# Retention loop: spreading the second split of the hidden planes over two tiles, and preparing the conv weights one tile earlier

## The chip, the cores and the metric

One core of one Trainium2 chip runs the kernel. The metric is device time in microseconds, the median of several executions. The engines are PE (TensorE, the matmuls), DVE (VectorE), ACT (ScalarE), POOL (GpSimd) and SP (SyncE, which here only issues DMAs). ACT issues some DMAs too. Each engine works through its own instructions in one fixed order; waits are semaphores.

## The reference, cut to what matters

One decoder layer on 2048 tokens of width 1024, in float32:

```python
mod = silu(c) @ ada_w + ada_b            # shift, scale, gate, two of each
h = x * (1 + scale_m) + shift_m
z = h @ w_in                              # 3*512 conv columns, 4*512 retention columns
y_conv = bg * conv3(cg * xin)             # short causal convolution
q, k = rotary(q), rotary(k) * d**-0.5     # 4 heads of 128, chunks of 128 tokens
y_ret = silu(g) * groupnorm(retention(q, k, v))
x = layernorm(alpha * x + gate_m * (concat(y_conv, y_ret) @ w_out))
h = x * (1 + scale_f) + shift_f
x = layernorm(alpha * x + gate_f * ((silu(h @ w_gate) * (h @ w_up)) @ w_down))
```

## The kernel before, in words

Float32 matmuls are made of fp16 ones. A helper `split` (L129 to L131) turns a float32 tile into a high and a low fp16 half: ACT writes the high half (L130), DVE the low one (L131). `mm3` (L135 to L137) makes one product of three fp16 matmuls, so most of PE's time has these three lines.

The retention half runs over 16 tiles of 128 tokens (`for t in range(4, NT)`; the first four tiles stand in the startup). `gemm_ret(t, u)` makes one of four column groups of 512 (v, q, k, gate) with 24 matmuls; its eviction from PSUM is DVE L709 for u = 0, ACT L713 for u = 1 and 2 and ACT L715 for u = 3. `evicted[0]` is the last of these, and `tc.issue_after(evicted[0])` asks that what follows is issued behind it. `rotary` is DVE L738 to L740 and POOL L741, L742. The split of q and k (L130/L131 `128x512`) feeds two DMA transposes on SP (L757), which the scores and the keys' products on PE need one tile later (`ret_scores`, `ret_kv`). `ret_y` and `ret_part` norm the output of a tile (DVE L804 to L814, POOL L808 to L811, L127).

Every second tile ACT modulates the next 256 tokens (`ret_h`, L296) and `ret_hsplit` splits them into a page of planes `h` (L130/L131 `hs`, `128x1024`). The convolution half multiplies the same tokens by a scheme with seven products in place of eight, which needs sums of the planes. `h_more` makes them: `h_sums` on POOL (L344 to L347, in place), a second `h_split` into a page `g`, and then seven stores to `hcscr` that ACT issues (`h_store`, L356). `h_again` does this for the first token pairs, whose x is loaded again. Both are `chores`, one taken at the end of a tile; the stores lie in a list and are taken behind `gemm_ret(t, 1)` of the next tile. The planes come back as `hp_load` (SP, L952).

The conv half runs in units n (`conv_pair`: products 0, 5, 4, 1, 3, 6, 2 of 12 matmuls each, evictions ACT L975 and L979 and DVE L977 to L988; L979 is `e5`). Its weights are loaded (`cw_load`, L862), their maximum taken (`cw_max`, DVE L87, PE L99, DVE L104), scaled (ACT L884), subtracted on POOL (L885 to L888) and split (ACT L892, DVE L893) in `cw_split`, for unit u + 1 while unit u runs. DVE L1166 adds two pages of `w_out`, which come by SP L1157.

In the startup `ret_half_max(0, 1)` is a maximum over 2048 columns (DVE L87 to `m`), and `start_bound` computes a bound `mh` (DVE L286, L87, L291) that PE L99 needs. Before the channel half, the last two rows of the output projection are normed (DVE L1276, L1277, POOL L1279 to L1286, ACT L1289) while `gu(0, 1)` starts; `gu_split2` prepares its weights (DVE L1435 to L1437, ACT L1440, DVE L1441), ACT L1478, L1483 and L1487 are its evictions, and DVE L1492 an addition from PSUM.

## Time and profile before

| | |
|---|---|
| time, median of 3 runs | 2091.64 us (2090.89 to 2095.92) |
| profiled execution | 2092.12 us, its span 2090.3 us |
| granted TensorE clock, mean | 0.99 |
| busy: PE, DVE, POOL, ACT | 96%, 70%, 43%, 32% |

The span is the time between the first and the last instruction that the profiler records; 1.8 us lie around it. A busy share is an average over stages that differ: it does not say which engine is waited for in one of them. A granted clock of 1.00 is 2.4 GHz, of 0.50 is 1.2 GHz.

### The profile page before, as it was taken

To read this page: it belongs to the slowest core of one execution; us is meant where nothing else is said; L and a number is where in the kernel's file an instruction comes from. 1 tells how busy PE (TensorE), PEld (TensorE's weight loads), DVE (VectorE), ACT (ScalarE), POOL (GpSimd) and SP (SyncE) were. 2 spreads that over 40 slices of the span, in tenths; PEclk is the share of its full clock that TensorE was granted. 3 is DMA by queue.
4 is the path that set the end of the run, shared out by engine and by line. 5 is a ranking of instruction groups with operands and counts; after the bars stand their busy time and mean duration, and the time that the engine had idled before them with its cause. 6 is when DMAs were issued, how large, how long until landed. Compare 5 with 4: busy or idle time off the path is not lost.

```text
span 2090.3 us, 24590 instructions
## 1 busy us (share of the span) xinstructions
PE 2017.0 (96%) x9631; PEld 945.5 (45%) x9631; DVE 1467.6 (70%) x1796; ACT 666.6 (32%) x728; POOL 897.0 (43%) x748
## 2 busy tenths in 40 slices
PE   8899998889899999899999999999999999999998
PEld 4355554444344444344444444444444444444443
DVE  7897766768677577867677677877877353477564
ACT  5523425334322223433232223433433121212210
POOL 3555546655642377644223115444444043134332
PEclk9999999999999999999999999999999999999999
DMA  9046553596774198742354543443343765465321
GB/s 382 26 137 187 157 171 121 147 317 208 269 287 151 66 258 189 192 132 91 142 187 155 191 181 121 166 136 131 130 154 125 251 254 193 149 259 196 147 81 71
DMA packets 189491, 361.05 MB, mean 173 GB/s; under 512 B 118080, under 2 KB 118080, under 8 KB 166592
## 3 DMA queue, kind: packets, MB, share of 16 engines
q1 hardware_dynamic: 181168, 344.55, 49.4%
q10 hardware_dynamic: 8208, 14.95, 2.0%
q8 instruction: 75, 1.23, 0.2%
q14 instruction: 40, 0.33, 0.0%
HBM read 231.26 MB, written 100.93 MB: 159 GB/s over the span
## 4 chain that ended last, share of the span: by engine, by line
PE 41%; DVE 9%; DMA 5%; POOL 4%; issue 2%; ACT 2%; SPq 0%; POOLq 0%; DVEq 0%; ACTq 0%
PE mm L135 7%; PE mm L137 7%; PE mm L136 7%; PE ax L135 7%; PE ax L137 7%; PE ax L136 7%; DMA pg<-yscr 2%; DMA pg<-in_w_dn_dram 2%; DVE pg L1639 1%; DVE pg L1504 1%; DVE wdm L87 1%; DVE pg L1441 1%; DVE pg L1640 1%; ACT pg L1289 1%; DVE pg L1499 1%
## 5 line engine op out<-in xcount | busy, mean ns | idle before, releaser
L135 PE MATMUL mm<-pg,pg 128*128 128x512 f16 x1604 | 609.0, 381 | 23.9 <-ACT pg L713 5.4
L136 PE MATMUL mm<-pg,pg 128*128 128x512 f16 x1604 | 611.1, 381 | 0.0
L137 PE MATMUL mm<-pg,pg 128*128 128x512 f16 x1604 | 609.8, 380 | 0.0
L135 PE MATMUL ax<-pg,pg 128*128 128x512 f16 x1220 | 463.2, 380 | 8.3 <-ACT pg L892 4.5
L136 PE MATMUL ax<-pg,pg 128*128 128x512 f16 x1220 | 463.2, 380 | 0.0
L137 PE MATMUL ax<-pg,pg 128*128 128x512 f16 x1220 | 462.1, 379 | 0.6 <-DVE pg L893 0.6
L136 PEld LDWEIGHTS <-pg 128*128 128x128 f16 x2888 | 283.5, 98 | 357.5 <-issue 31.4
L135 PEld LDWEIGHTS <-pg 128*128 128x128 f16 x2888 | 283.5, 98 | 343.8 <-ACT pg L892 11.6
L137 PEld LDWEIGHTS <-pg 128*128 128x128 f16 x2888 | 283.4, 98 | 341.4 <-issue 10.8
L1497 POOL TENSOR_TENSOR pg<-pg,t2k 128x512 f32<-128x512 f32 x44 | 59.9, 1362 | 385.4 <-DVE t2k L1496 219.8
L131 DVE SCALAR_TENSOR_TENSOR pg<-pg,p2s,pg 128x2048 f16<-128x2048 f32 (+1 forms) x42 | 93.1, 2225 | 137.5 <-ACT pg L130 137.4
L130 ACT ACTIVATE pg<-pg,p2s 128x2048 f16<-128x2048 f32 (+1 forms) x42 | 77.5, 1858 | 262.3 <-PE mm L136 105.1
L87 DVE TENSOR_REDUCE m<-pg 128x2 bf16<-128x2048 f32 (+1 forms) x38 | 86.4, 2276 | 16.1 <-DMA pg<-in_w_gu_dram 12.5
L528 PE MATMUL mm<-pg,pg 128*128 128x512 f16 x384 | 88.5, 384 | 5.7 <-DVE pg L536 2.5
L1503 ACT ACTIVATE pg<-t2k,ivg 128x512 f32<-128x512 f32 x44 | 31.6, 718 | 180.9 <-DVE t2k L1502 169.6
L1552 DVE TENSOR_TENSOR pg<-pg,pg 128x2048 f16<-128x2048 f32 (+1 forms) x22 | 46.3, 2104 | 44.5 <-ACT pg L1551 44.5
L1425 DVE TENSOR_TENSOR pg<-pg,pg 128x2048 f16<-128x2048 f32 x22 | 52.2, 2371 | 29.2 <-ACT pg L1424 29.2
L1551 ACT ACTIVATE pg<-pg 128x2048 f16<-128x2048 f32 (+1 forms) x22 | 37.3, 1697 | 99.7 <-DMA wscr<-pg 63.0
L1279 POOL TENSOR_SCALAR rs<-mv 128x1 f32<-128x1 f32 x32 | 30.2, 948 | 82.5 <-DVE mv L1277 79.8
L131 DVE SCALAR_TENSOR_TENSOR pg<-pg,hs,pg 128x1024 f16<-128x1024 f32 x32 | 50.2, 1593 | 18.4 <-ACT pg L130 18.3
L1605 POOL TENSOR_TENSOR pg<-pg,pg 128x2048 f32<-128x2048 f32 (+1 forms) x6 | 27.0, 4492 | 82.0 <-DVE pg L131 38.6
L528 PEld LDWEIGHTS <-pg 128*128 128x128 f16 x384 | 37.4, 99 | 52.0 <-issue 6.9
(283 smaller groups left out, 2766.8 us busy)
## 6 DMA issues: line engine op xcount, KB each, us to landing
pg<-wscr SPq DMA_DIRECT2D x28, 1024.0 KB, 4.9
pg<-in_w_gu_dram SPq DMA_DIRECT2D x22, 1024.0 KB, 4.9
uscr<-pg SPq DMA_DIRECT2D x44, 512.0 KB, 3.0
pg<-in_w_dn_dram SPq DMA_DIRECT2D x22, 1024.0 KB, 6.3
pg<-in_adaT_dram SPq DMA_DIRECT2D x21, 1024.0 KB, 8.1
wscr<-pg SPq DMA_DIRECT2D x77, 256.0 KB, 2.9
yscr<-pg SPq DMA_DIRECT2D x16, 1024.0 KB, 4.2
pg<-uscr SPq DMA_DIRECT2D x16, 1024.0 KB, 5.4
```

The source lines that it names most:

```text
L87: return nc.vector.tensor_reduce(dst, src, axis=AX.X, op=OP.max, apply_absolute_value=True).ins
L130: nc.scalar.activation(hi, src, AF.Copy, scale=s)
L131: nc.vector.scalar_tensor_tensor(lo, src, s, hi, op0=OP.mult, op1=OP.subtract)
L135: nc.tensor.matmul(ps, l_hi, r_hi, start=start, stop=False, skip_group_check=again)
L136: nc.tensor.matmul(ps, l_hi, r_lo, start=False, stop=False, skip_group_check=again)
L137: return nc.tensor.matmul(ps, l_lo, r_hi, start=False, stop=stop, skip_group_check=again).ins
L528: nc.tensor.matmul(ps, hv[:, a, k, o], w[:, k], start=n == 0 and k == k0, stop=n == 2 and k == k1 - 1)
L1425: nc.vector.tensor_sub(wa[:, 2048:], pg, wa[:, :2048])
L1497: nc.gpsimd.tensor_add(e5, e5, p1)
L1503: nc.scalar.activation(u[:, 1], u2, AF.Silu, scale=iv_g)
L1551: nc.scalar.activation(o[:, :n, 0], src, AF.Copy)
L1552: nc.vector.tensor_sub(o[:, :n, 1], src, o[:, :n, 0])
```

## The change

- `h_more` is cut into three steps. The sums stay at the tile's end. The second split moves into a list `sums`, taken behind the next tile's `gemm_ret(t, 1)` (after its latest eviction). The stores follow at the end of that tile, before the next chore.
- `cw_load(0)` and `cw_max(0)` move one tile earlier (tile 14), `cw_load(1)` with them. `cw_split` is cut behind the POOL subtractions; the rest, `cw_finish`, is called from within `conv_pair` behind the eviction `e5` of the unit before.
- In the startup `ret_half_max(0, 1)` moves behind the two `start_bound`.
- `gu_split2(1)` moves from the last rows of the output projection to behind `gu(0, 1)`, to be issued after the eviction `e5` (L1483).

```diff
@@ -381,18 +381,21 @@
         else:
             chores.append(lambda: h_more(p, pg, h))
 
-    chores, stores = [], []
+    chores, sums, stores = [], [], []
 
     def h_more(p, pg, h, *done):
         h_sums(pg)
-        g, _ = h_split(pg, hs[:, 0:1])
-        free(pg)
-
-        def store():
-            h_store(p, h, (0, 1, None, 3))
-            h_store(p, g, (5, 2, 6, 4))
-            free(g, *done)
-        stores.append(store)
+
+        def parts():
+            g, _ = h_split(pg, hs[:, 0:1])
+            free(pg)
+
+            def store():
+                h_store(p, h, (0, 1, None, 3))
+                h_store(p, g, (5, 2, 6, 4))
+                free(g, *done)
+            stores.append(store)
+        sums.append(parts)
 
     def h_again(p):
 
@@ -651,9 +654,9 @@
             ret_xmax(p, KG, KT)
         start_all(2, 0, (0,))
         start_mod(1)
-        ret_half_max(0, 1)
         start_bound(1, 0)
         start_bound(1, 1)
+        ret_half_max(0, 1)
         start_all(2, 0, (1,))
         start_scale(1, 0, lambda: start_x(1, 0))
         start_scale(1, 1, lambda: start_x(1, 1))
@@ -872,6 +875,8 @@
                 cw[u][m] = v[:, i]
         cw[u]["tmp"] = owner[id(pg)][1][:, 1536:2048]
 
+    cw_parts = {}
+
     def cw_split(u):
         pg = cw_stage.pop(u)
         s = col(1, "s")
@@ -886,6 +891,10 @@
         nc.gpsimd.tensor_sub(f[:, 1], f[:, 3], f[:, 1])
         nc.gpsimd.tensor_sub(sv[:, 1], f[:, 3], sv[:, 0])
         nc.gpsimd.tensor_sub(sv[:, 2], f[:, 2], sv[:, 1])
+        cw_parts[u] = (pg, f, sv)
+
+    def cw_finish(u):
+        pg, f, sv = cw_parts.pop(u)
         cw_views(u)
         for i, (src, n) in enumerate(((f, 4), (sv[:, :3], 3))):
             o = cw[u]["pages"][i].rearrange("p (s a n) -> p s a n", s=4, a=2)[:, :n]
@@ -951,7 +960,7 @@
         hp[b, m] = page(F16)
         nc.sync.dma_start(hp[b, m], hcscr[b][m].rearrange("p j m -> p (j m)"))
 
-    def conv_pair(u, b, done=lambda m: None):
+    def conv_pair(u, b, done=lambda m: None, between=None):
         w = cw[u]
         iv = ivc[:, u:u + 1]
         kind, c = CONV[u]
@@ -976,7 +985,10 @@
         prod(pb, 5, True, True)
         nc.vector.scalar_tensor_tensor(u2, pb, iv, p1, op0=OP.mult, op1=OP.add)
         prod(pc, 4, True, True)
-        nc.scalar.activation(e5, pc, AF.Copy, scale=iv)
+        read = nc.scalar.activation(e5, pc, AF.Copy, scale=iv).ins
+        if between:
+            with tc.issue_after(read):
+                between()
         prod(pa, 1, False, True)
         pd = new()
         prod(pd, 3, True, True)
@@ -1082,12 +1094,12 @@
         if t == 4:
             xt_load(p, 1)
         end = t == NT - 1
+        if t == NT - 2:
+            cw_load(0)
         ret_transpose(t - 1)
         gemm_ret(t, 0)
         if end:
             free(*ret_pages[0:2])
-            cw_load(1)
-            cw_max(0)
         if t > 4:
             ret_y(t - 2)
             ret_part(t - 2)
@@ -1095,8 +1107,8 @@
             ada_sum(t + 3)
         gemm_ret(t, 1)
         with tc.issue_after(evicted[0]):
-            while stores:
-                stores.pop()()
+            while sums:
+                sums.pop()()
         if t % 2 == 1 and p < 7:
             xt_load(p + 1)
         if t + 1 in AGAIN:
@@ -1106,6 +1118,7 @@
         if end:
             free(*ret_pages[2:4])
             cw_split(0)
+            cw_finish(0)
             cw_max(1)
             hp_load(0, 0)
             hp_load(0, 5)
@@ -1131,9 +1144,10 @@
             with tc.issue_after(evicted[0]):
                 ret_h(p)
                 ret_hsplit(p)
+        gemm_ret(t, 3)
         if t == NT - 2:
-            cw_load(0)
-        gemm_ret(t, 3)
+            cw_max(0)
+            cw_load(1)
         if end:
             free(*ret_pages[6:8])
             hp_load(0, 6)
@@ -1141,6 +1155,8 @@
         if t == 4:
             ret_mix(2)
         with tc.issue_after(evicted[0]):
+            while stores:
+                stores.pop()()
             if t in AGAIN:
                 h_again(AGAIN.index(t))
             elif chores:
@@ -1221,7 +1237,7 @@
             if n == 2:
                 ret_y(NT - 1)
                 free(spp)
-            conv_pair(u, b, done)
+            conv_pair(u, b, done, (lambda u=u: cw_finish(u + 1)) if n < 5 else None)
             if n == 0:
                 ret_transpose(NT - 1)
             if n == 2:
@@ -1449,7 +1465,7 @@
         gu_pages[0].append(wa)
         gu_pages[1].append(ws)
 
-    u32, ucount, gu_last, gu_pe, gu_act = [], [0], [None], [None], [None, None]
+    u32, ucount, gu_last, gu_pe, gu_act = [], [0], [None], [None], [None] * 3
     uscr = [[dram.tile([2, P, NCH, 512], F32, name=f"uscr{b}{r}") for r in range(2)] for b in range(2)]
     um = const.tile([P, 2, NFF], F32, name="um")
 
@@ -1480,7 +1496,7 @@
             prod(pb, "S2", T2, True, True)
             nc.vector.tensor_add(u2, pb, p1)
         prod(pc, "S1", T1_, True, True)
-        nc.scalar.activation(e5, pc, AF.Copy)
+        gu_act[2] = nc.scalar.activation(e5, pc, AF.Copy).ins
         if between:
             between()
         prod(pa, "A12", B21, False, True)
@@ -1703,7 +1719,6 @@
             free(*wo_pages[2:])
             for n in range(2):
                 gu_pages[n].append(page(F16, at=-1))
-            gu_split2(1, nc.vector)
         for t in (2 * j, 2 * j + 1):
             if i < 7:
                 op_half(t, 0)
@@ -1724,6 +1739,8 @@
         if i == 5:
             gu_load(1)
     gu(0, 1, late=True)
+    with tc.issue_after(gu_act[2]):
+        gu_split2(1, nc.vector)
     with tc.issue_after(gu_act[0]):
         gu_split1(1)
     with tc.issue_after(gu_act[1]):
```

ACT's instructions around the tile whose stall ends at 333.60 us: the last h splits (`pg<-pg,hs`) and evictions (L713, L715 before; L716, L718 after) of one tile, before:

```order
L296 ACTIVATE pg_78<-pg_78,mod,msc 128x256 x8
L130 ACTIVATE pg_89<-pg_78,hs 128x2x512 x2
L130 ACTIVATE pg_97<-pg_78,hs 128x2x512
L130 ACTIVATE t2k_2731<-pg_90,s_2726 128x512
L130 ACTIVATE pg_97<-pg_78,hs 128x2x512
L713 ACTIVATE pg_98<-mm_2776,iv_2222 128x512
L715 ACTIVATE pg_98<-mm_2825,iv_2222 128x512
```

and after:

```order
L296 ACTIVATE pg_83<-pg_83,mod,msc 128x256 x8
L130 ACTIVATE pg_78<-pg_83,hs 128x2x512 x2
L716 ACTIVATE pg_90<-mm_2732,iv_2215 128x512
L130 ACTIVATE pg_97<-pg_83,hs 128x2x512
L716 ACTIVATE pg_90<-mm_2769,iv_2215 128x512
L130 ACTIVATE pg_97<-pg_83,hs 128x2x512
L130 ACTIVATE pg_77<-pg_90,pg_88 128x512 x2
L130 ACTIVATE t2k_2727<-pg_82,s_2722 128x512
L718 ACTIVATE pg_90<-mm_2818,iv_2215 128x512
```

Before, the third h split and, behind the split of the retention output (`t2k`), the fourth stand ahead of all of these evictions; now an eviction stands ahead of each of the two.

DVE's instructions two tiles later, from the scores (L771 before, L774 after) to the next tile's first eviction (L709, L712), before:

```order
L771 SCALAR_TENSOR_TENSOR pg_82<-ax_3011,pg_88,mask 128x512
L786 TENSOR_TENSOR t2k_3030<-ax_3025,pg_88 128x512
L131 SCALAR_TENSOR_TENSOR pg_78<-pg_80,hs,pg_78 128x2x512 x2
L131 SCALAR_TENSOR_TENSOR pg_89<-pg_91,hs,pg_89 128x2x512 x2
L131 SCALAR_TENSOR_TENSOR pg_83<-pg_90,pg_88,pg_83 128x512 x2
L709 SCALAR_TENSOR_TENSOR pg_91<-mm_3089,iv_2616,cst 128x512
```

and after:

```order
L774 SCALAR_TENSOR_TENSOR pg_78<-ax_3004,pg_88,mask 128x512
L742 TENSOR_TENSOR pg_91<-pg_77,pg_86 128x8x64
L743 TENSOR_TENSOR pg_91<-pg_77,pg_86 128x8x64
L789 TENSOR_TENSOR t2k_3023<-ax_3018,pg_88 128x512
L131 SCALAR_TENSOR_TENSOR pg_94<-pg_89,hs,pg_94 128x2x512 x2
L131 SCALAR_TENSOR_TENSOR pg_91<-pg_77,pg_88,pg_91 128x512 x2
L131 SCALAR_TENSOR_TENSOR pg_83<-pg_82,hs,pg_83 128x2x512 x2
L712 SCALAR_TENSOR_TENSOR pg_97<-mm_3085,iv_2616,cst 128x512
```

Four h splits stood ahead of the q and k splits (`pg<-pg,pg,pg`); now two do, and two follow.

ACT's instructions at the end of the last retention tile and the start of the conv units, before (L892 is the weight split):

```order
L884 ACTIVATE pg_97<-pg_97,s_3699 128x2048
L892 ACTIVATE pg_80<-pg_77 128x4x512
L715 ACTIVATE pg_98<-mm_3671,iv_3046 128x512
L892 ACTIVATE pg_89<-pg_83 128x3x512
L892 ACTIVATE pg_86<-pg_97 128x4x512
```

and after (the weight split is L901, the eviction of the last column group L718, the stores L356):

```order
L889 ACTIVATE pg_91<-pg_91,s_3699 128x2048
L130 ACTIVATE pg_80<-pg_87,pg_88 128x512 x2
L901 ACTIVATE pg_76<-pg_78 128x4x512
L718 ACTIVATE pg_87<-mm_3664,iv_3039 128x512
L356 DMA hcscr_148<-pg_83 128x1024
L356 DMA hcscr_149<-pg_83 128x1024
L356 DMA hcscr_151<-pg_83 128x1024
L356 DMA hcscr_153<-pg_98 128x1024
L356 DMA hcscr_150<-pg_98 128x1024
L901 ACTIVATE pg_92<-pg_90 128x3x512
```

The scaling of the second unit's weights now runs ahead of the q and k splits, and five stores, which stood a tile's length earlier, stand between the two weight splits of the first unit.

## Rows read from the trace of the kernel before

**Rows 1.** The page's busy times.

```profile
PE 2017.0 (96%) x9631; PEld 945.5 (45%) x9631; DVE 1467.6 (70%) x1796; ACT 666.6 (32%) x728; POOL 897.0 (43%) x748
```

**Rows 2.** Timeline of PE, only matmuls with idle time before (in brackets, with releaser).

```profile
333.60 0.59 PE L135 MATMUL mm<-pg,pg 128*128 128x512 f16 x1 [5.41 <-ACT pg L713]
...
364.20 0.22 PE L135 MATMUL ax<-pg 128*128 128x128 f16 x1 [1.69 <-DMA pg<-pg]
...
387.61 0.26 PE L136 MATMUL ax<-pg 128*128 128x128 f16 x1 [5.49 <-DMA pg<-pg]
...
427.37 0.23 PE L99 MATMUL ax<-ident,m 128*128 128x128 f16 x1 [1.92 <-DVE m L87]
...
453.34 0.61 PE L135 MATMUL mm<-pg,pg 128*128 128x512 f16 x1 [3.41 <-ACT pg L892]
...
455.51 0.61 PE L135 MATMUL mm<-pg,pg 128*128 128x512 f16 x1 [1.13 <-ACT pg L892]
...
558.51 0.39 PE L135 MATMUL ax<-pg,pg 128*128 128x512 f16 x1 [2.64 <-ACT pg L892]
...
560.64 0.39 PE L135 MATMUL ax<-pg,pg 128*128 128x512 f16 x1 [1.53 <-ACT pg L892]
```

**Rows 3.** Windows: length, busy us of PE, PEld, DVE, ACT, POOL, granted clock, DMA.

```profile
332.60:339.40 6.80, 5.80 (x14) 2.07 (x14) 2.04 (x2) 6.08 (x12) 0.50 (x1) 0.50 0.75 143
340.00:365.00 25.00, 23.31 (x132) 12.73 (x131) 21.23 (x32) 10.39 (x16) 15.57 (x12) 1.00 0.48 162
452.00:458.90 6.90, 4.42 (x11) 1.28 (x12) 5.58 (x6) 3.35 (x3) 1.94 (x3) 0.51 1.15 266
561.30:564.70 3.40, 3.40 (x9) 1.21 (x8) 2.32 (x3) 0.00 (x0) 2.47 (x3) 0.50 0.86 284
```

**Rows 4.** Timeline of ACT before the first stall.

```profile
327.89 1.15 ACT L130 ACTIVATE pg<-pg,hs 128x1024 f16<-128x1024 f32 x1 [7.19 <-POOL pg L345]
```

**Rows 5.** Timeline of DVE before the stall at 382; figures of L131, all splits.

```profile
371.70 6.99 DVE L131 SCALAR_TENSOR_TENSOR pg<-pg,hs,pg 128x1024 f16<-128x1024 f32 x4 [0.89 <-ACT pg L130]
378.62 3.43 DVE L131 SCALAR_TENSOR_TENSOR pg<-pg,pg,pg 128x512 f16<-128x512 f32 x2
...
L131 DVE SCALAR_TENSOR_TENSOR pg<-pg,hs,pg x29: 1270/1286/2390, 221.4 to 428.4; 128x1024 f16<-128x1024 f32 x29
L131 DVE SCALAR_TENSOR_TENSOR pg<-pg,pg,pg x18: 735/1510/1753, 231.5 to 448.4; 128x512 f16<-128x512 f32 x18
```

**Rows 6.** Timelines of DVE and ACT at the first conv weights.

```profile
425.02 2.29 DVE L87 TENSOR_REDUCE m<-pg 128x1 bf16<-128x2048 f32 x1 [1.34 <-DMA pg<-in_w_conv_dram]
...
451.38 1.91 ACT L892 ACTIVATE pg<-pg 128x2048 f16<-128x2048 f32 x1 [1.93 <-POOL pg L886]
```

**Rows 7.** Stores: the line's figures, and six in a row on ACT.

```profile
L356 ACTq DMA_DIRECT2D hcscr<-pg x56: 326/453/2041, 222.8 to 441.4; - x56
...
DMA to landing us min/median/max: 2.4/4.4/14.0
...
365.82 4.65 ACTq L356 DMA_DIRECT2D hcscr<-pg x6
```

**Rows 8.** Timeline of DVE in conv unit 5.

```profile
544.04 2.67 DVE L1166 TENSOR_TENSOR pg<-pg,pg 128x2048 f32<-128x2048 f32 x1 [7.09 <-DMA pg<-in_w_out_dram]
```

**Rows 9.** Timelines of PE and DVE at the start of `gu(0, 1)`.

```profile
883.75 0.38 PE L135 MATMUL mm<-pg,pg 128*128 128x512 f16 x1 [2.90 <-ACT pg L1483]
891.42 0.38 PE L135 MATMUL mm<-pg,pg 128*128 128x512 f16 x1 [1.89 <-DVE t2k L1492]
...
887.80 2.97 DVE L1353 TENSOR_TENSOR pg<-pg,pg 128x512 f32<-128x512 f32 x3 [1.36 <-ACT pg L1289]
```

**Rows 10.** Timelines of PE and DVE in the startup.

```profile
58.72 0.29 PE L99 MATMUL ax<-ident,mh 128*128 128x128 f16 x1 [5.53 <-DVE mh L291]
55.92 2.28 DVE L87 TENSOR_REDUCE m<-pg 128x1 bf16<-128x2048 f32 x1
66.71 2.35 DVE L451 SCALAR_TENSOR_TENSOR pg<-pg,s,pg 128x2048 f16<-128x2048 f32 x1 [2.07 <-ACT pg L445]
```

## The prediction

> **What bounds the kernel now.** The page gives PE 96% of the span [rows 1], so time can come only from PE's idle time and from stretches in which its granted clock is low. I read PE's timeline first, for matmuls that stood idle and what released them [rows 2], then the windows behind these places, for the clock [rows 3], and then, for each place, the timeline of the engine that was late. What [rows 2] shows: the regions that the change touches hold four stalls in the retention tiles (5.41, 1.69, 5.49, 1.92 us), two at the first conv unit (3.41, 1.13) and two at unit 5 (2.64, 1.53). What [rows 3] shows: behind a stall the clock can fall from 2.4 to 1.2 GHz for a few microseconds. Behind the one at 333.6 the granted clock is 0.50 for 6.8 us, of which PE worked 5.80: 2.9 us lost at half speed. In the one from 452.0 PE worked 4.42, 2.2 lost; in the one from 561.3 it worked 3.40, 1.7 lost; the two others of that length, after 387.6 and 427.4, cost by the same row up to 1.7 each, and I take 1.5 and 1.7, since the first begins with the end of its stall.
>
> **The second split of the planes.** The stall at 333.6 ends with an eviction on ACT, which stood behind h splits, and the third of these waited 7.19 us for POOL's sums [rows 4]. PE had no free PSUM tile. The first order excerpt shows that evictions now pass between those splits, and the splits are issued a whole column group later than the sums. A column group is 24 matmuls, and 9631 of them in 2017.0 us are 0.21 each [rows 1]: 5 us, so some 2 us of the 7.19 stay, before an eviction that is due only then. I take the whole 5.41 and the 2.9 of clock: 8.3. The lower end is 2 us less.
>
> The stalls at 364.2 and 387.6 wait for DMA transposes, and these wait for the q and k splits. Before the second, DVE did four h splits in 6.99 us and then the two q and k splits in 3.43 [rows 5]. The second excerpt shows two h splits ahead now. By the shortest of [rows 5] two h splits are 2.54 us, so the transposes are issued at least that much earlier, and by the measured pair 3.5; the rest of the 5.49 has to come from the sums, which no longer run beside the q and k splits: 3.43 less twice the shortest 0.735 is 2.0. Together 4.5 to 5.5; I take 5.49 and 1.5 of clock, 7.0, and 1.69 for the stall before it. Sum of the three: 17.0.
>
> A rule of the Trainium skill bears on this (SBUF — State Buffer, section "SBUF: two separate sides"): VectorE and GpSimd share one pair of SBUF ports, and whichever of a GpSimd operation and a VectorE operation with two SBUF inputs starts first holds it while the other is blocked. The spread of one shape in [rows 5], 0.735 to 1.753 us, agrees.
>
> **Stores.** Moved, not changed in number: seven per pair of tiles, 0.453 us each at the median and 0.78 in a row of six [rows 7], so 3.2 to 5.4 us of ACT's queue, ahead of eight modulations and two h splits in every second tile. The next column group's eviction is due two groups later, about 10 us, and ACT is busy 10.39 of 25 us in [rows 3]. I price this at 0; its upper end is a rival below.
>
> **Conv weights.** The maximum waited for its load (the DVE row at 425.02), and PE for the maximum [rows 2, 6]. A tile earlier the load has four column groups, 20 us, more. That removes 1.92 and 1.7 of clock: 3.6.
>
> At the first conv unit the third excerpt speaks against a gain. The two weight splits on ACT had one eviction between them; the first ran at 451.38 for 1.91, and PE waited for each [rows 2, 6]. Now five stores stand between, 2.3 to 3.9 us by [rows 7]. The scaling moved only little, since it stands behind the same evictions. If the first split comes earlier than before by as much as the stores take, nothing changes; if not at all, the second is up to 3.9 later, but 1.13 of that was waited before. I take a loss of 1.7, with ends of 3.3 lost and 6.7 won (3.41 + 1.13 + 2.2, all stalls gone).
>
> At unit 5, DVE stood 7.09 us for `w_out` [rows 8], and the scale of the next weights behind it; PE then waited 2.64 and 1.53 for these. Now the scaling is ahead of L1166, and the splits a unit early. I take both and the clock: 5.9. The load of `w_out` is issued no earlier, so DVE may stand there again with an addition for PE behind it; between 0 and those 2.64.
>
> **The startup.** `mh` comes 2.28 us earlier, since the maximum stands behind it now [rows 10]; the 5.53 shrink to about 3.2. But DVE does the same work until L104 of that maximum, and DVE at 66.71 had waited for ACT's L445, which waits for that scale, so PE is held there again. 0, with ends of 1.0 won (a clock that stays up) and 1.7 lost (a clock that falls later).
>
> **The channel weights.** The 2.90 at 883.75 goes, since the eviction L1483 no longer stands behind the copy L1440. But the next stall, 1.89 at 891.42, waits for DVE's L1492, which stands behind additions (L1353) that wait for the last rows' norm (ACT L1289) [rows 9], and by the code that waits for POOL and DVE, whose order there is the same as before. So PE arrives 2.9 earlier and waits about 4.8 there. I take 0, with 1.7 lost if the clock falls behind the longer stall.
>
> **Sum.** 17.0 + 3.6 − 1.7 + 5.9 = 24.8. A stall removed lets the next one show: before, 1.69 appeared a tile behind 5.41, and 5.49 a tile behind that. I take one stall of the small size with its clock as left somewhere, 1.69 + 1.7 = 3.4. That leaves 21.4. The profiled execution took 2092.1, 0.5 above the median shown, so 2070.7; I say 2071.
>
> **Rivals.**
> Half of it goes to the shared port. DVE and POOL together are busy 36.8 us in the 25 of [rows 3]. The sums now lie beside the work at the tile's start (rotary and the h splits of the other page), and if these stretch as the q and k splits did (1.51 median for 0.735), the transposes are late again by 3.9 us (1.9 from four h splits, 2.0 from two q and k splits) in three tiles: 24.8 − 3 × 3.9 = 13.1, or 2079. For it: the spread. Against it: DVE has 15% free there. By the Trainium skill's rule above (SBUF — State Buffer, "SBUF: two separate sides") every overlap of a sum with such a DVE operation would block one of the two, which is this rival at its full size.
>
> The change does not do what it says: the stall moves to the transposes. A page that held h is reused for the next transposes, so these wait for h splits that now come up to a tile later. Three stalls of 5.5 in place of the three, 16.5 given back, and the first conv unit at its worst: 24.8 − 16.5 − 1.6 is 6.7, or 2085; with their clock nothing is left, 2092. For it: two of the three stalls were already such waits. Against it: the second excerpt.
>
> Slower: the stores block the next evictions. They now start at the tile's end, and the page that they read becomes the next tile's q, k, v page, so its first eviction on DVE, about 5 us later, waits for them to land. Four stores of 0.78 and a landing of 4.4 are 7.5, late by 2.5, which other column groups may hide, as PE has PSUM tiles left; a landing of 14.0 [rows 7] is late by 12, and rotary, splits and transposes stand behind it on DVE. It decides from a landing of about 10 us on in most tiles. Then four tiles lose 5.5 each, and the 17.0 aren't won: 2092 + 22 − 7.8 is 2106.
>
> **Chances.** The forecast (2060 to 2077) 0.53; the first conv unit cured as well (to 2059) 0.05; half to the port (2077 to 2085) 0.17; the stall moved (2085 to 2098) 0.15; slower 0.10. 0.3%, 6.3 us, is about what a measurement of this kernel can tell from no change. Faster by more 0.75, within 0.15, slower by more 0.10. The forecast's own range is 2060 to 2080. For 8 in 10 the low end is the best case: 26.5 without the loss at the first conv unit and without the rest, with 6.7 there, is 33.2, 2059. The high end goes into the moved stall, 2091.
>
> **What would show it.** In the changed profile: no idle time on PE over 2 us between 320 and 430 us, the granted clock 1.00 there; ACT's h splits without a wait for L345; PE waiting some 4 to 6 us for the weight split at the first conv unit; nothing over 1 us at unit 5; a stall of 4 to 5 us for L1492 near 870. It would be wrong if transposes or the first evictions show as releasers in tiles 7 to 15, or if the stores land late.

## The result, and the profile after

The changed kernel is slower: 2109.85 us at the median of five runs (2103.68 to 2111.46) against 2091.73 of the kernel before (2090.89 to 2095.92), ratio 1.0075 (1.0064 to 1.0087). The forecast was 2071, with 2091 as its high end.

The profiled execution took 2103.68 us, the fastest of the five, so its trace holds 11.6 of the 18.1 us; the clock and the stalls of the other four are not seen one by one. Its page, to be read beside [rows 1]:

```profile
PE 2021.0 (96%) x9631; PEld 947.7 (45%) x9631; DVE 1468.2 (70%) x1796; ACT 666.2 (32%) x728; POOL 906.9 (43%) x748
```

The span went from 2090.3 to 2101.9 us, 11.6 more. PE is busy 4.0 us longer with the same 9631 matmuls, which goes with the lower mean clock (0.988 for 0.990), and idle for the other 7.6 (80.9 against 73.3). How far each kernel is, by the windows of PE alone (length, busy us and matmuls, granted clock, DMA share, GB/s), before and then after:

```profile
0.00:400.00 400.00, 365.78 (x1897) 0.98 0.54 169
400.00:470.00 70.00, 63.12 (x333) 0.93 0.82 262
```

```profile
0.00:400.00 400.00, 368.32 (x1896) 0.97 0.52 161
400.00:470.00 70.00, 52.53 (x269) 0.91 0.75 224
```

At 400 us the two kernels are level: new stalls have cost there what the old ones gave back. The loss of this execution appears between 400 and 470 us, in the last two retention tiles and the first conv unit, where 64 matmuls fewer are done. Where the idle time lies, in the timeline of PE (the view of [rows 2] and [rows 9]):

```profile
66.72 0.59 PE L531 MATMUL mm<-pg,pg 128*128 128x512 f16 x2 [2.10 <-ACT pg L448]
...
278.56 0.22 PE L136 MATMUL ax<-pg 128*128 128x128 f16 x1 [2.68 <-DMA pg<-pg]
...
308.34 0.27 PE L136 MATMUL ax<-pg 128*128 128x128 f16 x1 [3.84 <-DMA pg<-pg]
...
362.01 0.29 PE L135 MATMUL ax<-pg 128*128 128x128 f16 x1 [2.79 <-DMA pg<-pg]
...
421.74 0.39 PE L135 MATMUL mm<-pg,pg 128*128 128x512 f16 x1 [1.10 <-DVE pg L712]
...
429.96 0.80 PE L800 MATMUL ax<-pg,pg 128*128 128x128 f32 x2 [2.86 <-DVE g L123]
...
449.56 0.22 PE L99 MATMUL ax<-ident,m 128*128 128x128 f16 x1 [3.81 <-DVE pg L817]
...
464.45 0.61 PE L135 MATMUL mm<-pg,pg 128*128 128x512 f16 x1 [4.24 <-ACT pg L901]
469.41 0.61 PE L135 MATMUL mm<-pg,pg 128*128 128x512 f16 x1 [3.92 <-ACT pg L901]
...
554.50 0.39 PE L135 MATMUL mm<-pg,pg 128*128 128x512 f16 x1 [2.56 <-ACT pg L901]
...
904.68 0.59 PE L135 MATMUL mm<-pg,pg 128*128 128x512 f16 x1 [3.82 <-DVE t2k L1508]
```

The four old stalls of the retention tiles are gone. In their place stand six up to 450 us, and the three between 270 and 365 us are released by DMA transposes of q and k. The clock falls behind them, as it fell behind the old ones [rows 3]; a window, with the columns of [rows 3] (0.57 from 361 to 369 us):

```profile
306.00:312.00 6.00, 3.66 (x21) 3.18 (x21) 6.00 (x12) 0.00 (x0) 1.79 (x2) 0.56 0.32 64
```

Each of these three stalls ends when one transpose lands. The DMA view of the single microseconds from 269.5, 297.3 and 353.0 us shows the one issued there, with its time from issue to landing at the end of the row:

```profile
pg<-pg SPq DMA_TRANSPOSE x1, 8.7
...
pg<-pg SPq DMA_TRANSPOSE x1, 10.9
...
pg<-pg SPq DMA_TRANSPOSE x1, 8.9
```

SP's timeline has the same three with their time of issue:

```profile
269.78 2.04 SPq L760 DMA_TRANSPOSE pg<-pg  x1
...
297.42 2.89 SPq L760 DMA_TRANSPOSE pg<-pg  x1
...
353.12 5.56 SPq L760 DMA_TRANSPOSE pg<-pg  x1
```

Issue plus landing is 278.5, 308.3 and 362.0, within a tenth of the times at which PE starts again. A landing of 3.1 us, the shortest that this line has, would have been over at 272.9, 300.5 and 356.2, each ahead of the time at which PE began to wait (275.9, 304.5, 359.2). So these transposes are not issued late, they take long. What was under way beside the second, by the DMA view of 290 to 310 us (busy tenths in 40 slices; queue, packets, MB, share; issues):

```profile
DMA  9300698999999999979999999997999999920000
...
q1 hardware_dynamic: 3512, 3.21, 58.3%
q10 hardware_dynamic: 1008, 1.84, 27.0%
...
hcscr<-pg ACTq DMA_DIRECT2D x7, 256.0 KB, 6.0
mrscr<-pg SPq DMA_DIRECT2D x1, 1024.0 KB, 5.8
pg<-in_adaT_dram SPq DMA_DIRECT2D x1, 1024.0 KB, 8.5
pg<-pg SPq DMA_TRANSPOSE x2, 8.6
```

q10 carries ACT's DMAs, here the seven stores, and q1 SP's. From 292.5 to 307.5 us the DMA engines are nearly full; the transpose lands at 308.3. The stores are not all of it: SP's own queue, with the transposes, a load and a store of 1 MB, takes twice their share. In the kernel before, a transpose issued at 287.27 landed after 7.5 us with q1 alone at work; no matmul waited for that one. Over all 18 transposes, before (L757) and after (L760), from 215 to 480 us:

```profile
L757 SPq DMA_TRANSPOSE pg<-pg x18: 1231/1337/3618, 231.7 to 453.2; - x18
DMA to landing us min/median/max: 3.0/4.3/8.3
```

```profile
L760 SPq DMA_TRANSPOSE pg<-pg x18: 1232/1770/5562, 233.0 to 479.6; - x18
...
DMA to landing us min/median/max: 3.1/6.3/10.9
```

The median landing after is twice the shortest. Counted transpose by transpose: before, 14 of the 18 have on average less than one store under way over their first 3 us; after, 3 of the 16 up to 470 us. The Trainium skill (DMA: Bandwidth & Descriptors, section "Queues, rings and completion order") says that SP and ACT each own one row of rings on the same 16 DMA engines, and that an engine takes turns, packet by packet, between the rows that have work. As an estimate from that, with packets of both rows taking equally long, a transpose beside a stream of stores gets half of each engine, 6.2 us for 3.1; the median of 6.3 is near it, the 8.7 to 10.9 of the three stalls are longer. The turns themselves no view here shows.

Behind 400 us several things meet. Of the stores: ACT's evictions of q and k stood in four places, three of them behind 400 us and the longest 9.29 us at 444.57, for stores of their page that had not landed (what ended L716's idle time, us and times); and POOL stood for a transpose that landed in 7.0 us (its timeline), on which by POOL L814 and DVE L817 the stall at 449.56 hangs:

```profile
  DMA hcscr<-pg: 17.6, 4
```

```profile
444.79 1.15 POOL L763 TENSOR_TENSOR pg<-pg 128x512 f32<-128x512 f16 x1 [9.16 <-DMA pg<-pg]
```

Of the order on SP: DVE stood for the first conv weights. Timelines of DVE and SP:

```profile
403.93 1.48 DVE L131 SCALAR_TENSOR_TENSOR t2k<-pg,s,t2k 128x512 f16<-128x512 f32 x1 [0.19 <-ACT t2k L130]
414.06 2.29 DVE L87 TENSOR_REDUCE m<-pg 128x1 bf16<-128x2048 f32 x1 [8.65 <-DMA pg<-in_w_conv_dram]
```

```profile
405.44 1.62 SPq L839 DMA_TRANSPOSE pg<-t2k  x1
407.17 2.28 SPq L865 DMA_DIRECT2D pg<-in_w_conv_dram  x2
```

This load was not slow: it landed 6.9 us after its issue, as against 6.3 before. It was issued late, because on SP it stands behind a transpose that waits for DVE's split of the retention output, the last thing that DVE did before it stood. The stalls at 421.74 and 429.96 follow: the tile's first eviction (L712) and its rotary stand behind this maximum on DVE.

### The profile page after: what moved, and what is told of

Read it like the earlier page. It is cut to its first block, busy times and chain, and to the rows that moved or that the text cites. A ratio compares the mean times of both kernels' runs of the same rounds, so it can differ in the third digit from the quotient of the medians.

```text
span 2101.9 us, 24591 instructions
## 1 busy us (share of the span) xinstructions
PE 2021.0 (96%) x9631; PEld 947.7 (45%) x9631; DVE 1468.2 (70%) x1796; ACT 666.2 (32%) x728; POOL 906.9 (43%) x748
## 3 DMA queue, kind: packets, MB, share of 16 engines
q1 hardware_dynamic: 181168, 344.55, 49.2%
## 4 chain that ended last, share of the span: by engine, by line
PE 43%; DVE 9%; POOL 4%; DMA 4%; issue 2%; ACT 2%; SPq 0%; POOLq 0%; DVEq 0%; ACTq 0%
PE ax L135 8%; PE ax L136 7%; PE ax L137 7%; PE mm L135 7%; PE mm L136 7%; PE mm L137 7%; DMA pg<-in_w_dn_dram 2%; DMA pg<-yscr 1%; ACT pg L1305 1%; DVE wdm L87 1%; DVE pg L1457 1%; DVE pg L1520 1%; POOL pg L1370 1%; POOL rs L1295 1%; DVE pg L1335 1%
## 5 line engine op out<-in xcount | busy, mean ns | idle before, releaser
L135 PE MATMUL mm<-pg,pg 128*128 128x512 f16 x1604 | 610.0, 382 | 21.8 <-ACT pg L901 10.7
L135 PEld LDWEIGHTS <-pg 128*128 128x128 f16 x2888 | 283.9, 98 | 347.4 <-ACT pg L901 12.2
L131 DVE SCALAR_TENSOR_TENSOR pg<-pg,p2s,pg 128x2048 f16<-128x2048 f32 (+1 forms) x42 | 92.7, 2216 | 137.8 <-ACT pg L130 137.7
L1568 DVE TENSOR_TENSOR pg<-pg,pg 128x2048 f16<-128x2048 f32 (+1 forms) x22 | 46.3, 2104 | 44.6 <-ACT pg L1567 44.6
L1370 POOL TENSOR_TENSOR pg<-pg,pg 128x512 f32<-128x512 f32 x32 | 46.5, 1474 | 29.1 <-DVE pg L1369 26.9
```

The costliest lines, as they stand in the source:

```text
L131: nc.vector.scalar_tensor_tensor(lo, src, s, hi, op0=OP.mult, op1=OP.subtract)
L135: nc.tensor.matmul(ps, l_hi, r_hi, start=start, stop=False, skip_group_check=again)
L1370: nc.gpsimd.tensor_add(v[:, c], v[:, c], rows[:, D + n * 512:D + (n + 1) * 512])
L1568: nc.vector.tensor_sub(o[:, :n, 1], src, o[:, :n, 0])
```

## The experiments

Theory: the stores' new place, the tile's end, puts them beside the next transposes, and these land late because both share the DMA engines. First rival: the time is ACT's, whose queue holds the stores ahead of evictions. Second rival: the loss is in another part, the first conv unit above all. One caution holds for every run: the kernel leaves the order of the instructions on each engine to a scheduler (`schedule_with_timeline_sim=True` at its end), and an edit of a few lines can change that order elsewhere too. Differences below are from the median of the kernel before in runs of the same time (2094.75 for e1 to e4, 2094.46 for e5 to e8, 2094.37 for e9 to e12, 2094.16 for e13 to e15, 2095.96 for e16 and e17).

**The parts alone.** e1 is the kernel before with the planes' three steps only, e2 the changed kernel without them:

```diff
 e1, against before
-        stores.append(store)
+            stores.append(store)
+        sums.append(parts)
...
         with tc.issue_after(evicted[0]):
+            while stores:
+                stores.pop()()
             if t in AGAIN:
 e2, against the changed kernel: these lines the other way round
```

> The kernel before with the three-step planes alone (sums, splits behind the next tile's gemm_ret(t, 1), stores at that tile's end). Theory A (the stores now land beside the tile's DMA transposes and delay them): new stalls for transposes at about 276, 304 and 359 us and the old ones at 333, 364 and 387 gone, retention loop some 5 us slower or equal, conv stalls as before; total 2093 to 2102. Theory B (the loss is the conv weights' new order, the planes as such win): faster than before by 8 to 17 us, 2075 to 2084.

> The changed kernel with the three-step planes undone (startup, conv weights a tile ahead and gu_split2 stay). Theory A: most of the loss gone, no transposes as releaser but those of before, total 2086 to 2096. Theory B: as slow as the changed kernel or slower, 2100 to 2110.

e1: 2116.56, 21.8 slower (ratio 1.0102, 1.0087 to 1.0117). e2: 2089.44, 5.3 faster (0.9969, 0.9957 to 0.9981). The whole loss is in the planes. The three other parts, alone on the kernel before:

```diff
 e6: the conv part
+        if t == NT - 2:
+            cw_load(0)
         ret_transpose(t - 1)
...
+        if t == NT - 2:
+            cw_max(0)
+            cw_load(1)
...
-            conv_pair(u, b, done)
+            conv_pair(u, b, done, (lambda u=u: cw_finish(u + 1)) if n < 5 else None)
 e7: the channel weights
-            gu_split2(1, nc.vector)
...
+    with tc.issue_after(gu_act[2]):
+        gu_split2(1, nc.vector)
 e8: the startup
-        ret_half_max(0, 1)
         start_bound(1, 0)
         start_bound(1, 1)
+        ret_half_max(0, 1)
```

> The kernel before with the conv weights' part alone (a tile ahead, cw_finish behind e5). Theory A and my forecast's terms (3.6 at the first maximum, 5.9 at unit 5, first unit unchanged as the stores are not moved here): 5 to 9 us faster, 2083 to 2088. Rival E (the gain of the kernel without the planes came from the startup): within 3 us of before.

> The kernel before with gu_split2(1) moved alone. My forecast: the 2.90 us stall goes and the next one grows by as much, 0 to 2 us slower by the clock, 2091 to 2095. Rival: 2 to 4 us faster.

> The kernel before with ret_half_max(0, 1) moved alone. My forecast: the 5.53 us stall shrinks to 3.5, PE waits later for the same DVE and ACT work, -1 to +2 us. Rival E: 2 to 4 us faster.

e6: 2086.64, 7.8 faster (0.9958, 0.9944 to 0.9971). e7: 2096.89, 2.4 slower (1.001, 1.0001 to 1.0019). e8: 2094.98, no difference (1.0002, 0.9992 to 1.0011). The parts add up: 21.8 − 7.8 + 2.4 + 0.5 = 16.9, where the whole change has 18.1. As an edit the second rival falls: the loss comes with the planes. As a place in time it does not fall: e1 too is level at 400 us (1900 matmuls) and loses between 400 and 470 us (261 for 333).

**The stores' place.** e3 moves only the stores of the kernel before to the tile's end and leaves sums and splits where they were. e4 keeps the changed kernel and moves only the stores, from the tile's end to behind `gemm_ret(t, 2)`:

```diff
 e3, against before
-        with tc.issue_after(evicted[0]):
-            while stores:
-                stores.pop()()
...
         with tc.issue_after(evicted[0]):
+            while stores:
+                stores.pop()()
             if t in AGAIN:
 e4, against the changed kernel
         gemm_ret(t, 2)
+        with tc.issue_after(evicted[0]):
+            while stores:
+                stores.pop()()
...
-            while stores:
-                stores.pop()()
             if t in AGAIN:
```

> The kernel before with one edit: the seven stores move from behind gemm_ret(t, 1) to the tile's end; sums and splits stay together at the tile end before. Theory A: slower than before by 5 to 15 us, transposes land 6 to 10 us after their issue where stores run beside them (3.2 us before), new stalls for transposes. Rival C (the stores' place does not matter, the splits' later place delays what DVE does for q and k): within 4 us of before, stalls where they were.

> The changed kernel with the stores one column group earlier, behind gemm_ret(t, 2) in place of gemm_ret(t, 3), half a tile from the transposes' place. Theory A: transposes land in 3 to 4 us again, stalls at 276, 304 and 359 gone, 6 to 14 us faster than the changed kernel, 2092 to 2103. Rival C: as the changed kernel, 2104 to 2111.

e3: 2107.11, 12.4 slower (1.0059, 1.0042 to 1.0077). e4: 2087.89, 6.9 faster (0.9969, 0.9957 to 0.998), where the changed kernel is 18.1 slower: 25.0 between them. In e3 the time came out as the theory has it, but only in part the way. The median of the transposes' landings is 4.4 us, as before; PE stands for two of them, 1.94 us at 401 and 5.92 at 349.16, where the view names no releaser but a transpose issued at 343.24 lands 0.1 us earlier, after 5.8 us with stores beside it. The largest stall, 8.16 us at 446.80, is for DVE's maximum of the conv weights. DVE's and SP's timelines of e3, and SP's of the kernel before:

```profile
444.46 2.29 DVE L87 TENSOR_REDUCE m<-pg 128x1 bf16<-128x2048 f32 x1 [10.36 <-DMA pg<-in_w_conv_dram]
```

```profile
430.27 1.29 SPq L836 DMA_TRANSPOSE pg<-t2k  x1
...
436.34 1.74 SPq L862 DMA_DIRECT2D pg<-in_w_conv_dram  x2
```

```profile
418.66 0.33 SPq L862 DMA_DIRECT2D pg<-in_w_conv_dram  x1
```

The load lands 8.1 us after its issue, 1.8 later than before, but it is issued 17.7 us later, behind transposes that in the kernel before come after it. And its execution is 44 matmuls behind at 230 us (1027 for 1071), ahead of its first store at 240.6. So much of e3's loss comes from a changed order of instructions, and the 12.4 are not the price of stores beside transposes alone.

e4 beats what was expected of it in time, but three stalls for transposes are left (3.10, 1.69 and 2.23 us at 352, 380 and 407 us), and their median landing is 4.8 us, not 3 to 4. By 400 us it has done 1945 matmuls where the changed kernel has 1896, so the stores' place is what eats the gain up to there. Its longest stall is the stores' too: in the last tile four of them stand on ACT ahead of L889, and they wait for loads from `hcscr` to land. PE's and ACT's timelines of e4:

```profile
455.17 0.61 PE L135 MATMUL mm<-pg,pg 128*128 128x512 f16 x1 [11.57 <-ACT pg L901]
```

```profile
441.94 8.11 ACTq L356 DMA_DIRECT2D hcscr<-pg  x4
450.09 2.00 ACT L889 ACTIVATE pg<-pg,s 128x2048 f32<-128x2048 f32 x1 [10.90 <-DMA pg<-hcscr]
```

e5 takes the second group of first token pairs one tile earlier, so that the last tile has no stores; e9 is what the experiments point to, the conv part of e6 with the planes as in e5, and startup and channel weights as before:

```diff
-    AGAIN = (7, 10, 11, 13)
+    AGAIN = (7, 9, 11, 13)
```

> The changed kernel with the stores behind gemm_ret(t, 2) as in the run before, and the second of the four repeated page loads one tile earlier (tile 9 for 10), so that no chore and no store is left for the last retention tile. Theory A (stores beside other DMAs cost; in the last tile they stood behind the loads of the conv planes and held ACT's weight splits for 11 us): the stall of 11.57 us at 443 falls to 4 to 5, 5 to 9 us faster than with the stores moved alone, 2078 to 2084. Rival D (that stall is the conv weights' own chain through POOL): it stays over 8, within 3 us of 2088.

> The kernel before with the conv weights' part, the three-step planes with the stores behind gemm_ret(t, 2) and the repeated page load at tile 9; startup and gu_split2 as before. If the parts add (conv weights -8, planes at that place -3 to -5, gu_split2 +2 left out), 2080 to 2084, 5 us at most below the run with all parts.

e5: 2084.21, 10.3 faster (0.9947, 0.9934 to 0.9961); the long stall is gone, but that is 3.4 beyond e4 where 5 to 9 was expected. e9: 2082.57, 11.8 faster (0.9938, 0.9925 to 0.9951), and beats both kernels. Its transposes land in 3.7 us at the median, and what is left of idle time over 1 us in its retention tiles is four waits at L800, of 1.60, 1.12, 1.20 and, in PE's timeline,

```profile
419.98 0.49 PE L800 MATMUL ax<-pg,pg 128*128 128x128 f32 x2 [2.84 <-DVE g L123]
```

**More stores, other issuers.** e11 and e12 issue each store twice (the second writes the same bytes to the same place), in the kernel before and in the changed one; e10 lets POOL issue the stores of the changed kernel:

```diff
 e11, e12
                 nc.scalar.dma_start(hcscr[p // 4][m][:, p % 4], v[:, q])
+                nc.scalar.dma_start(hcscr[p // 4][m][:, p % 4], v[:, q])
 e10
-                nc.scalar.dma_start(hcscr[p // 4][m][:, p % 4], v[:, q])
+                nc.gpsimd.dma_start(hcscr[p // 4][m][:, p % 4], v[:, q])
```

> The changed kernel with its stores issued by POOL in place of ACT, at the same place in the program. Theory A (stores and transposes share the DMA engines, whoever issues them): transposes beside stores still land in 6 us or more, stalls for transposes stay, time 2104 or slower. Rival F (the stores held ACT's queue, and the evictions and splits behind them made the transposes late): the stalls go, 2088 to 2098.

> The kernel before with each store issued twice in a row with the same data; place as before. Theory A in the form that place decides: transposes away from the stores land in 3.2 us as before, 0 to 6 us slower. In the form that the amount of bytes alone decides: 10 to 20 us slower.

> The changed kernel with each store issued twice. Theory A: transposes beside the stores land later still, 9 to 14 us at the median (6.3 with one store each), 10 to 30 us slower than the changed kernel. Rival C (the splits' place, not the stores): 0 to 4 us slower than the changed kernel.

e11: 2110.11, 15.7 slower (1.0071, 1.0054 to 1.0088), a miss for "the place alone": twice the stores at the old place cost nearly as much as once at the other. There too the transposes release PE, 7.04 us in one stall. e12: 2126.23, 31.9 slower (1.0156, 1.0139 to 1.0174), 13.8 more than the changed kernel. Amount and place both count. The median landing is no measure of it: 4.2 in e11 and 5.9 in e12, where 9 to 14 was expected. What grew is the time that PE waits for transposes: 14.9 in e11 for 7.4 before, 18.7 in e12 for 10.0 in the changed kernel. e10: 2092.20, 2.2 faster (0.9986, 0.9978 to 0.9995), 20.3 from the changed kernel. That is the time that the first rival expected, not the theory (2104 or slower); but POOL reaches its stores between its own work and so spreads them, and two things change at once: the transposes land in 5.3 us, and ACT is rid of the issues. It does not tell the theory from the first rival.

**Extra stores or extra ACT time.** From here on work is added to e9. e13 and e14 add at the end of tiles 7 to 14 seven stores of 256 KB to scratch that nobody reads, issued by POOL and by ACT; e15 adds there 24 small copies on ACT, time without bytes:

```diff
+            if 6 < t < NT - 1:
+                for i in range(7):
+                    nc.gpsimd.dma_start(dscr[(t - 7) * 7 + i], ret_w[3][0][:, :2])
 e14: nc.scalar.dma_start in its place
 e15
+                for i in range(24):
+                    nc.scalar.activation(dact, ret_w[3][0][:, 0, :32], AF.Copy)
```

> The best kernel (e9) with seven more stores of the same size at the end of each of tiles 7 to 14, of a resident page to scratch memory, issued by POOL. Bytes (theory A): transposes beside them land in 5 us and more, 10 to 25 us slower than that kernel (2092 to 2108). ACT's queue (F): within 4 us of it.

> The same seven stores at the same place, issued by ACT. Theory A: about as slow as with POOL's, plus 0 to 5. F: 10 to 25 us slower than the best kernel, where POOL's cost nothing.

> The best kernel with 24 small copies on ACT (about 0.2 us each, some 4.8 us) at the end of each of tiles 7 to 14 and no more stores. Theory A: within 4 us of the best kernel. F: 8 to 20 us slower.

e13: 2106.31, 12.2 slower (1.0049, 1.0028 to 1.007), and inconclusive. What they read is ready early, nothing ties them to a tile, and the line's figures show all 56 in the startup:

```profile
L1164 POOL DMA_DIRECT2D dscr<-pg x56: 539/539/805, 92.1 to 176.7; - x56
```

e14: 2106.64, 12.5 slower (1.0052, 1.0031 to 1.0072), 24 more than e9. ACT's stores stand in place, the transposes land in 4.6 us at least, 7.7 at the median and 13.2 at most, and the longest stall on PE's timeline in these tiles, 7.31 us at 284.41, is for a transpose.

e15: 2079.33, 14.8 faster (0.9922, 0.9904 to 0.994), no slower than e9: this much of ACT's time at that place costs nothing. It is not the issue time on ACT. Whether ACT's queue costs in another way, by holding evictions until stores land, needs the same stores from POOL, tied to their tile. e16 and e17 add them so, reading a column group of the tile:

```diff
+                for i in range(7):
+                    nc.gpsimd.dma_start(dscr[(t - 7) * 7 + i], qp[t][:, 1536:])
 e17: nc.scalar.dma_start in its place
```

> The best kernel (e9) with seven more stores of 256 KB at the end of each of tiles 7 to 14, of what the tile's last eviction wrote, issued by POOL. Theory A (bytes on the shared DMA engines): transposes beside them land in 5 us and more at the median, and 10 us or more slower than the best kernel. F (the waits of ACT's queue behind stores): transposes may land late, but less than 6 us slower than the best kernel.

> The same seven stores, issued by ACT. Both theories: some 20 us slower than the best kernel, as with the unbound stores by ACT. Under A within 8 us of the run with POOL's, under F at least 12 us slower than that.

e16: 2105.23, 9.3 slower than before (1.0049, 1.0033 to 1.0064), 21 more than e9. e17: 2113.14, 17.2 slower (1.0067, 1.0046 to 1.0089), 29 more. The same bytes cost 21 from POOL, which rules out that ACT's queue is all of their cost, and 29 from ACT. The 7.9 between them lie at the theory's edge (8) and short of the first rival's 12; what they are was not tried. In e16 the cost is seen directly; figures of the transposes with who waited for them:

```profile
L760 SPq DMA_TRANSPOSE pg<-pg x18: 1233/2346/8047, 236.6 to 470.3; - x18
...
  PE ax L135: 11.8, 5
  PE ax L136: 9.7, 6
...
DMA to landing us min/median/max: 3.1/6.9/16.6
```

PE itself stood 21.5 us for transposes (11.8 + 9.7), two of the stalls 6.05 and 6.17 long, where in e9 it stood 1.6; by 400 us e16 has done 1873 matmuls, e9 1947. The profiled executions are 26.4 us apart (2110.03 and 2083.61), so this is three quarters of it, and the half clock behind such stalls comes on top. In e17 (the same line's figures) the landing has nearly the same median, and PE waits less for it, but ACT stands for it, and PE's stalls are mostly at L800, which waits for DVE (seven, 20.8 us):

```profile
  ACT pg L130: 19.0, 3
  PE ax L136: 5.3, 2
...
DMA to landing us min/median/max: 3.2/6.4/11.5
```

## Why the prediction was wrong

**The step that failed** is the one on the stores: "Moved, not changed in number" and "I price this at 0; its upper end is a rival below". It counted what seven issues take of ACT's queue and asked which eviction is due next on ACT. e15 shows that this part was right: ACT had room for it. It left out what the 256 KB of each store do on the DMA engines, and which transfer is issued next. Behind `gemm_ret(t, 1)` the stores ran mostly between two sets of transposes, at the tile's end beside or just ahead of one. The place costs 25.0 us (the changed kernel against e4), not 0. The sign named for it came: transposes are the releasers, and the stores themselves land in 6.1 us at the median for 4.4 before. Up to 400 us the way is shown: the transposes land late and PE stands for them, and the gain of the second split is gone. Behind 400 us the stores of the last tile and the changed order on SP act together, and no run parts them. e3's 12.4 can't stand for the place, since much of it is lost before its first store and to a load issued late.

The kernel before had the sign of it. The transpose whose landing ended its stall of 5.49 us was issued at 382.07 us, as soon as DVE's splits were done, and seven stores were being issued beside it; timelines of SP and ACT before:

```profile
382.07 1.48 SPq L757 DMA_TRANSPOSE pg<-pg  x1
```

```profile
378.81 3.77 ACTq L356 DMA_DIRECT2D hcscr<-pg  x7
```

It landed in 5.5 us, 2.5 above the shortest of its line, so by its landing too, and not by the splits on DVE alone, that stall was as long as it was.

**Its two rivals on the other side.** "The stall moves to the transposes" named the right releaser with 0.15, for a wrong reason: it had the transposes wait for h splits in a reused page, and so be issued late; they are issued in time and land late. "The stores block the next evictions" had the sign, the time (2106) and the place, with 0.10. It foresaw the landing as the quantity that decides, but for an eviction on DVE in four tiles, 5.5 us each; the trace has one such wait, 3.5 us (L712), and on ACT the 17.6 us of L716. So its time came out near by luck.

**The second split.** The old stalls at 333, 364 and 387 went, as said, and ACT's wait for the sums with them. But 17.0 less the 3.4 of rest, 13.6, was too much for the whole kernel even with the stores in a better place: e9 is 4.0 faster than e6, and e5 4.9 faster than e2. e6 has stalls of 5.69, 2.41 and 4.16, 12.3 us, in these tiles, e9 seven over 0.3 that add up to 8.3, mostly at L800 (`ret_y`), which waits for DVE. So the rest that shows after a stall is gone was mis-sized: 8.3 of idle time, not 1.69. That is not the whole of it. These stalls are short, and the clock stays up (1.00 from 230 to 400 us, 0.97 in e6): e9 does 906 matmuls in this stretch and e6 829, 77 more, some 16 us at the forecast's 0.21 each (an estimate). It falls back behind it, 307 for 338 from 400 to 470 us, with 3.88 and 2.18 at the first conv unit for e6's 3.53 and 1.13. So in the tiles the gain was about there, and a good part of it was lost again at the conv weights behind them. Why e9 does worse there was not tried.

**The conv weights.** 3.6 − 1.7 + 5.9 is 7.8, and e6, without the planes, measured 7.8. That they agree to the tenth is luck, since the terms were not each right: in e6 the maximum waits no longer, the first unit keeps its two stalls (3.53 and 1.13), so no loss there, and unit 5 loses its own, but a stall of 2.23 stands elsewhere. In the changed kernel the 3.6 for the first maximum did not come: "A tile earlier the load has four column groups, 20 us, more" took its issue for given, but SP issued it at 407.17, 11.5 us earlier than before and not 20, and DVE, where the maximum now stands, waited 8.65 for it; in e6 it was issued at 395.35. The first unit has 4.24 and 3.92 for 3.41 and 1.13, 3.6 worse and so beyond the worst end, 3.3; the second split there does not wait for the five stores ahead of it, as I argued, but 2.91 us for a subtraction on POOL:

```profile
467.87 1.48 ACT L901 ACTIVATE pg<-pg 128x1536 f16<-128x1536 f32 x1 [2.91 <-POOL pg L893]
```

Of unit 5's two stalls 2.56 and 0.94 are left in the changed kernel.

**The startup and the channel weights.** Much as predicted: the `mh` stall shrank (3.46 for 5.53) and PE was held again, 2.10 for ACT's L448, with no gain (e8). At `gu(0, 1)` the 2.90 went and L1508 holds PE 3.82, a little under the 4 to 5 that were said; e7 measures 2.4 lost, a little over the 1.7 of the lower end.

**The half to the port.** The trace speaks against it: DVE's q and k splits, 1.510 us at the median before [rows 5], are 0.742 after (220 to 450 us), so what should have grown shrank, and the stalls up to 365 us wait for transfers. It was not tried by itself.

**What stays open.** Between 400 and 470 us the shares of the last tile's stores, of the late load and of the order of the weight splits are not told apart. The profiled execution explains 11.6 us; why the four other runs are 5 to 8 us longer still was not followed. In e13 the same bytes in the startup cost 24, and why so much there was not tried.

## What to carry to other kernels

A DMA that is moved is moved on the DMA engines too. Look at its new place for the transfer that is issued next and is soon needed, and take that one's landing beside other traffic from the trace, not its shortest; a median of 4.3 with a maximum of 8.3 before the change already said that this line is sensitive. When a load is waited for, look first at when it was issued: here one that landed in 6.9 us held DVE 8.65, because it stood on its queue behind a transfer that waited for DVE. Before an execution's loss is laid to its most striking stalls, count how far each kernel is at a few times. And of several stalls in a row, expect removing them to uncover the next engine's: here 12.3 us of idle time gave way to 8.3, mostly waits for DVE.

## What the runs showed that I had not expected

A transpose of q or k lands in 3.0 us at best, in 6.3 to 7.7 at the median where stores of 256 KB stand beside it (the changed kernel, e14, e16, e17), and in up to 16.6 us (e16); beside SP's own transfers of 1 MB alone it took 7.5 us (before, at 287.27). And that although the queues take only 51.7% of the DMA engines over the span (49.2, 2.3 and 0.2 on the changed kernel's page).

24 extra copies on ACT per tile end cost nothing: 2079.33 (2078.27 to 2081.31) against e9's 2082.57 (2078.77 to 2084.68). The 3 us less are hardly the copies' doing: in the profiled executions e15 is ahead at 230 us, 1070 matmuls for 1045, and the first copy runs at 234.8.

A DMA whose source is ready early and that is bound to nothing may run far ahead of where the code has it: the stores of e13, written at the ends of tiles 7 to 14, ran from 92 to 177 us.
